# The branch for crowded experts goes into the loop of the experts, and the last expert's loads and down product are rearranged

## The chip, the cores and the metric

The kernel runs on one core of one Trainium2 chip. Its time is the device time of one execution, in microseconds (us). The time before is 2425.18 us, the median of 3 runs from 2423.32 to 2428.69. One further execution was recorded by the hardware profiler; it took 2428.05 us, and all durations below come from it.

The core has a matrix engine (PE, TensorE; its weight loads are PEld), VectorE (DVE), ScalarE (ACT), GpSimd (POOL) and SyncE (SP). SP computes nothing here: it issues nearly all DMA transfers, in the order of its program. A transfer that must wait (for a free buffer, say) holds back all that stand behind it on SP.

## The reference, cut to what matters

Two models of two layers run in one launch: a hybrid stack (recurrent and sparse attention, then multi-head latent attention, each with an mlp) on `x`, and two decoder layers on the second set of inputs (256 tokens, width 1024). What the change touches is the mixture of experts at the end of each decoder layer:

```python
def hier_moe(h, ...):          # 256 tokens, 32 experts in 4 groups, 2 experts per token
    ...                        # group by argmax, top 2 experts inside it, weights
    def expert_block(args):    # for the tokens of one expert e
        xb, e = args
        return (jax.nn.silu(xb @ w_exp_gate[e]) * (xb @ w_exp_up[e])) @ w_exp_down[e]
    ...
    return out                 # weighted sum over each token's two experts

x = x + gate2 * hier_moe(modulate(rms_norm(x), shift2, scale2))   # end of a layer
```

`w_exp_gate` and `w_exp_up` are 1024x512 per expert, `w_exp_down` 512x1024, all in float32: 2 MB each, 6 MB per expert, 192 MB per layer. The next layer begins with an rms norm of `x`, and after the second layer a final rms norm gives the output.

## The kernel before, in words

The experts are walked in order, 0 to 31. For each, up to 64 of its tokens are gathered beforehand (`xg`), and all 64 columns are computed whether they are filled or not. An expert that has more than 64 tokens is "crowded": a tensor `most` (the largest count) says whether there is one, and `crowded` (L1961) holds a loop over all experts for the tokens beyond the first 64, inside `tc.If(n > 64)` (L1967). Each engine loads the count into a register (L1966) and branches by itself. On the inputs timed here the body is not entered: the engines jump over it. Before the change this branch stands at the end of `moe`, behind everything else of the layer.

A weight matrix comes as two loads of 1 MB (128 partitions x 2048 numbers), issued by SP in `xload` (L1765, the DMA is at L1770). `xtile` deals out 17 buffers in turn: 7 called `xw`, 7 called `w`, 3 called `xw2`. So each load has to wait until PE has used the tile that was loaded 17 loads earlier, and for one of eight DMA semaphores (DMAHW0 to 7). The order of the loads is gate 0, up 0, and then for each expert e: gate e, down e-1, up e; at the end down 31. Counted from 0 in each layer, the loads of gate e, down e-1 and up e have the numbers 6e-2 to 6e+3.

PE's work per expert, in its program order: the gate product (`expert_in`, L1792, 32 passes for a matrix), the down product of the expert before (`expert_out`, L1816, 16 passes over 512 columns), the up product (L1792 again), `combine` (L1957, eight products that add the expert's output to four accumulators in PSUM), and two small transposes (`choice`, L1780; `expert_act`, L1804). Behind the down product ACT copies each half of the result out of PSUM (L1821) and DVE takes the rest of it to a second part (L1822); the two column halves c = 0 and 1 lie in one PSUM bank, in partitions 0 to 63 and 64 to 127.

At the end of a layer, in a block whose order is kept as written (`self.ordered()`), stand the last down product, its combine, the update of `x` (DVE, L1946), its squares (ACT, L1949), their sums (PE, L1950), and the scale of the next norm (`rstd_sums`, L461 to L471: a copy, a small product, a square root, a reciprocal). Then comes the branch, and then the next norm's first product (L478), which makes the scale available to all partitions.

Of the kernel before, what the change touches and what calls it, by code (L numbers as in the profile page):

```python
# [9 lines left out]
FT = mybir.dt.float32  # L10
FR = mybir.dt.float32r
# [3 lines left out]
AF = mybir.ActivationFunctionType  # L15
OP = mybir.AluOpType
# [4 lines left out]
T = 256  # L21
# [92 lines left out]
def layout(a):  # L114

    g = {}
# [5 lines left out]
    w = a["hy_w_in"][0]  # L122
    xr, yr, q, k, v, iq, ik, iw = np.split(w, np.cumsum([512, 512, 512, 64, 64, 256, 64])[:7], axis=1)
# [42 lines left out]
    for n, kc in (("w_exp_gate", 4), ("w_exp_up", 4), ("w_exp_down", 2)):  # L166
        g[n] = rowwise(a[n + "_2"], kc, 2048 // kc)[:, :, :, 0]
# [17 lines left out]
class Prog:  # L185
# [1579 lines left out]
    def xload(self, ap, kc, n):  # L1765

        half = []
        for h in range(2):
            t = self.xtile()
            self.nc.sync.dma_start(t, ap[h])  # L1770
            half.append(t.rearrange("p (c n) -> p c n", n=n))
        return lambda k: half[k // (kc // 2)][:, k % (kc // 2)]
# [36 lines left out]
    def expert_out(self, ht, wd):  # L1809

        nc = self.nc
        py = self.bank()
        for n in range(4):
            h, b = n // 2, n % 2
            for c in range(2):
                nc.tensor.matmul(py[64 * c:64 * c + 64], ht[:, b * 128 + h * 64:b * 128 + h * 64 + 64],  # L1816
                                 wd(2 * h + b)[:, c * 512:(c + 1) * 512], start=n == 0, stop=n == 3)
        y = self.t4("ey", FR)
        for c in range(2):
            p, n = py[64 * c:64 * c + 64], slice(c * 512, (c + 1) * 512)  # L1820
            nc.scalar.activation(y[:64, n], p, AF.Copy)  # L1821
            nc.vector.tensor_tensor(y[64:, n], p, y[:64, n].bitcast(FT), op=OP.subtract)  # L1822
        return y

    def moe(self, l):
# [88 lines left out]


        state = None
        for e in range(32):
            if e % G == 0:
                if e:
                    oh = onehot(e // G)  # L1920
                    xg = gather(oh, [[(k2, part)] for k2 in range(4) for part in range(2)])
                wohs = weighted(e // G, oh)
            xs = lambda k, xg=xg, a=e % G * 64: xg[k // 4][:, k % 4, a:a + 64]
            wg = self.xload(g["w_exp_gate"][l, e], 8, 512)
            ps = self.bank()
            self.expert_in(ps, 0, xs, wg)
            if state:
                wd = self.xload(g["w_exp_down"][l, e - 1], 4, 1024)
                y = self.expert_out(state[0], wd)
            wu = self.xload(g["w_exp_up"][l, e], 8, 512)  # L1930
            self.expert_in(ps, 256, xs, wu)
            if state:
                for j in range(8):
                    self.combine(acc, j, y, state[1], e == 1)
            ct, sw = self.choice(wohs[e % G])
            state = self.expert_act(ps, sw), ct
        gate = self.modc[:, l, 40:48]
        wd = self.xload(g["w_exp_down"][l, 31], 4, 1024)
        with self.ordered():
            self.table(AF.Sqrt, state[0][:, :1])  # L1940
            y = self.expert_out(state[0], wd)
            for j in range(8):
                self.combine(acc, j, y, state[1], False, True)
            sums = self.bank()
            for j in range(8):
                ve.scalar_tensor_tensor(self.x[j], acc[j // 2][:, (j % 2) * T:(j % 2 + 1) * T], gate[:, j:j + 1],  # L1946
                                        self.x[j], op0=OP.mult, op1=OP.add)
                sq = self.t1("rsq")
                sc.activation(sq, self.x[j], AF.Square)  # L1949
                te.matmul(sums[32 * (j % 4):32 * (j % 4) + 32, :T], self.ones[:, :32], sq, start=j < 4, stop=j >= 4)  # L1950
# [11 lines left out]
    def crowded(self, l, tok, posm, wt, most, gate, modulate):  # L1962
# [3 lines left out]
        n = nc.values_load(most[0:1, 0:1], min_val=0, max_val=T)  # L1966
        with tc.If(n > 64):  # L1967
            ev = self.sm.tile([128, 1], FT, name="ev", tag="ev", bufs=1)
            ve.memset(ev, 0.0)
            with tc.For_i(0, 32, 1) as e:  # L1970
                wts = []
                for n, kc, c in (("w_exp_gate", 4, 512), ("w_exp_up", 4, 512), ("w_exp_down", 2, 1024)):
                    half = []
                    for h in range(2):
                        w = self.ring.tile([128, 2048], FT, name="xw", tag="xw").rearrange("p (c n) -> p c n", c=kc)
                        rows = g[n][l, bass.ds(e, 1), h]
                        nc.sync.dma_start(w, rows.rearrange("e p (c n) -> p (e c) n", c=kc))
                        half.append(w)
                    wts.append(lambda k, half=half, kc=kc: half[k // kc][:, k % kc])
# [8 lines left out]
                for b in range(1, T // 64):  # L1988
# [20 lines left out]
                    for o in range(2):  # L2009
                        self.expert_in(ps, o * 256, lambda k: xg[:, k], wts[o])  # L2010
# [9 lines left out]
            self.rstd_tokens(self.squares(self.x), 8, 1e-6, out=self.r)  # L2020
# [129 lines left out]
```

## Time and profile before

| What | Before |
|---|---|
| Median of 3 runs | 2425.18 us (2423.32 to 2428.69) |
| Profiled execution | 2428.05 us, span 2426.2 us |
| PE busy | 2287.1 us (94%) |
| DVE, ACT, POOL busy | 1146.2 (47%), 868.7 (36%), 200.3 us (8%) |
| Moved by DMA | 658.71 MB, 272 GB/s over the span |
| Expert loop, layer 0 | about 1122 to 1566 us of the span |
| Expert loop, layer 1 | about 1958 to 2404 us of the span |

The shares are means over the whole program. The page also shows the span in 40 slices; in the slices of the two expert loops the DMA engines are busy 90% or more of the time at 420 GB/s, elsewhere mostly between 30 and 70%. So the two loops have to be read by themselves, and the rows further down do that. The time in the rows is that since the start of the span.

### The profile page before, as it was taken

Reading aid. Unit: us, or ns where it says so; the run is one execution under the profiler, and the core shown is the slowest. Engines: PE = TensorE matmul, PEld = TensorE weight load, DVE = VectorE, ACT = ScalarE, POOL = GpSimd, SP = SyncE. Lnnn points to the kernel's source line nnn. Section 1 sums busy time; section 2 is a strip of 40 time slices with the busy share of each in tenths; the row PEclk is TensorE's granted clock in tenths of the full one; section 3 lists DMA queues with packets and bytes.
Section 4 is the critical chain, followed back from the end, with each engine's and each line's share of the span. In section 5 each row is a group of like instructions: output and inputs, shape, how many; then the busy total and the mean of one; then the engine's idle time right before and its main releaser. Section 6 shows DMA issues by size and latency. Waiting matters only on the chain. (4 is left out here: it accounts for less than half of the span.)

```text
span 2426.2 us, 45869 instructions
## 1 busy us (share of the span) xinstructions
PE 2287.1 (94%) x19846; PEld 1816.3 (75%) x19846; DVE 1146.2 (47%) x1864; ACT 868.7 (36%) x1415; POOL 200.3 (8%) x171
## 2 busy tenths in 40 slices
PE   7899999999998999998889999889999988999996
PEld 7689997799997899986555565478989855565653
DVE  6775566665555756653222222258566432222222
ACT  4654445554445533442111221244335321121111
POOL 5110000010000101010000000010010100000000
PEclk9999999999999999999999999989999999999999
DMA  7745555555556534367999999955333679999996
GB/s 267 297 161 176 190 200 208 194 208 190 177 189 236 207 123 131 108 266 281 420 420 420 420 420 420 417 194 178 135 120 127 258 320 420 420 420 420 420 420 260
DMA packets 93315, 658.71 MB, mean 272 GB/s; under 512 B 10416, under 2 KB 11824, under 8 KB 14128
## 3 DMA queue, kind: packets, MB, share of 16 engines
q1 hardware_dynamic: 91376, 652.14, 69.3%
q10 hardware_dynamic: 1728, 3.54, 0.4%
q8 instruction: 159, 2.61, 0.4%
q14 instruction: 52, 0.43, 0.1%
HBM read 654.59 MB, written 1.05 MB: 270 GB/s over the span
## 5 line engine op out<-in xcount | busy, mean ns | idle before, releaser
L336 ACT ACTIVATE wh<-w 128x1024 fp32r<-128x1024 f32 x359 | 380.4, 1060 | 562.8 <-PE bank L353 494.3
L339 DVE TENSOR_TENSOR wl<-w,wh 128x1024 fp32r<-128x1024 f32 x330 | 420.1, 1274 | 334.3 <-ACT wh L336 333.4
L352 PE MATMUL bank<-hh,wh 128*128 128x256 f32 x1568 | 454.4, 290 | 0.0
L354 PE MATMUL bank<-hh,wl 128*128 128x256 f32 x1568 | 444.4, 283 | 3.5 <-DVE wl L339 3.5
L353 PE MATMUL bank<-hl,wh 128*128 128x256 f32 x1568 | 443.9, 283 | 0.0
L352 PEld LDWEIGHTS bank<-hh,wh 128*128 128x128 f32 x1568 | 300.7, 192 | 11.2 <-issue 7.9
L354 PEld LDWEIGHTS bank<-hh,wl 128*128 128x128 f32 x1568 | 301.0, 192 | 4.9 <-DVE wl L339 4.9
L353 PEld LDWEIGHTS bank<-hl,wh 128*128 128x128 f32 x1568 | 301.2, 192 | 1.1 <-issue 1.0
L1792 PE MATMUL bank<-xw,xg 128*64 128x256 f32 x2464 | 282.6, 381 | 2.3 <-SPq L1967 2.2
L1792 PEld LDWEIGHTS bank<-xw,xg 128*64 128x64 f32 x2464 | 173.3, 137 | 109.5 <-issue 22.9
L1822 DVE TENSOR_TENSOR ey<-bank,ey 64x512 fp32r<-64x512 f32 x128 | 88.2, 689 | 259.1 <-ACT ey L1821 259.1
L1792 PE MATMUL bank<-w,xg 128*64 128x256 f32 x1632 | 188.6, 381 | 5.4 <-DMA w<-in_w_exp_up_dram 5.4
L1792 PEld LDWEIGHTS bank<-w,xg 128*64 128x64 f32 x1632 | 114.2, 137 | 77.3 <-issue 13.8
L1821 ACT ACTIVATE ey<-bank 64x512 fp32r<-64x512 f32 x128 | 75.8, 592 | 264.1 <-PE bank L1816 216.4
L1785 DVE TENSOR_SCALAR ct<-cs 128x256 fp32r<-128x256 f32 x64 | 20.2, 316 | 304.2 <-ACT cs L1783 304.1
L1783 ACT ACTIVATE cs<-bank 128x256 f32<-128x256 f32 x64 | 24.5, 383 | 343.6 <-PE bank L1780 343.6
L1816 PE MATMUL bank<-xw,eh 128*64 128x512 f32 x608 | 143.2, 597 | 2.3 <-DVE eh L1806 1.0
L352 PE MATMUL bank<-rh,wh 128*128 128x256 f32 x512 | 144.9, 283 | 0.0
L353 PE MATMUL bank<-rl,wh 128*128 128x256 f32 x512 | 144.9, 283 | 0.0
L354 PE MATMUL bank<-rh,wl 128*128 128x256 f32 x512 | 144.9, 283 | 0.0
L1858 POOL TENSOR_TENSOR woh<-oh,wt 128x256 f32<-128x256 f32 x64 | 37.4, 615 | 750.0 <-PE bank L1792 526.1
L1816 PE MATMUL bank<-w,eh 128*64 128x512 f32 x416 | 97.9, 597 | 1.4 <-DMA w<-in_w_exp_down_dram 1.2
(526 smaller groups left out, 3885.5 us busy)
## 6 DMA issues: line engine op xcount, KB each, us to landing
xw<-in_w_exp_up_dram SPq DMA_DIRECT2D x78, 1024.0 KB, 17.3
xw<-in_w_exp_gate_dram SPq DMA_DIRECT2D x76, 1024.0 KB, 15.3
xw<-in_w_exp_down_dram SPq DMA_DIRECT2D x76, 1024.0 KB, 19.6
w<-in_mlp_w_dram SPq DMA_DIRECT2D x64, 1024.0 KB, 4.9
w<-in_w_exp_down_dram SPq DMA_DIRECT2D x52, 1024.0 KB, 17.1
w<-in_w_exp_gate_dram SPq DMA_DIRECT2D x52, 1024.0 KB, 15.9
w<-in_w_exp_up_dram SPq DMA_DIRECT2D x50, 1024.0 KB, 15.6
w<-in_w_ada_dram SPq DMA_DIRECT2D x48, 1024.0 KB, 4.9
```

The source lines that it names most:

```text
L336: nc.scalar.activation(hv, src, AF.Copy)
L339: (nc.gpsimd if fresh or pool else nc.vector).tensor_tensor(lv, src, hv.bitcast(FT), op=OP.subtract)
L352: te.matmul(out, a, xh[x0 + k], start=start and k == 0, stop=False, skip_group_check=True)
L353: te.matmul(out, a, xl[x0 + k], start=False, stop=False, skip_group_check=True)
L354: te.matmul(out, b, xh[x0 + k], start=False, stop=stop and k == kc - 1, skip_group_check=True)
L1783: nc.scalar.activation(s, pc[:, :T], AF.Copy, accum_out=w)
L1785: nc.vector.tensor_scalar(ct, s, 0.0, None, op0=OP.not_equal)
L1792: self.nc.tensor.matmul(ps[64 * h:64 * h + 64, o:o + 256], xk(k), w(k)[:, h * 256:(h + 1) * 256], start=k == 0 and o == 0, stop=k == 7, sk ...
L1816: nc.tensor.matmul(py[64 * c:64 * c + 64], ht[:, b * 128 + h * 64:b * 128 + h * 64 + 64], wd(2 * h + b)[:, c * 512:(c + 1) * 512], start=n ...
L1821: nc.scalar.activation(y[:64, n], p, AF.Copy)
L1822: nc.vector.tensor_tensor(y[64:, n], p, y[:64, n].bitcast(FT), op=OP.subtract)
L1858: nc.gpsimd.tensor_tensor(woh[:, i, :, c], oh[:, i].bitcast(FT), wt[:, i, es, None].to_broadcast([128, G, 64]), op=OP.mult)
```

## The change

The order of the loads is made by a list, and `weights()` takes the next pair of tiles from it. For expert 31 the order is gate, up, down 30, down 31 instead of gate, down 30, up, down 31.

After the combine of expert 9, SP first issues loads ahead until `turn` is a multiple of 17 (loads 58 to 67 of that layer), and then comes `crowded`, in the middle of the loop. Its buffers are taken out of the same pools ahead of the branch. It no longer computes the scale of the next norm itself.

The down matrices are stored so that one 1 MB tile holds 512 of the 1024 output columns for all of the inner dimension, where before it held half of the inner dimension for all columns. The down product is made of 32 passes over 256 columns instead of 16 over 512, one column half f after the other. For the last expert of a layer each half f is copied out, combined and added to `x` by itself. Both halves f lie in one PSUM bank.

```diff
-    def expert_out(self, ht, wd):
+    def expert_out(self, ht, wd, combine=None, add=None):
         py = self.bank()
-        for n in range(4):
-            h, b = n // 2, n % 2
+        pv = py.rearrange("p (f n) -> p f n", f=2)
+        y = self.t4("ey", FR)
+        yv = y.rearrange("p (f c n) -> p f c n", f=2, c=2)
+        def out(c, f):
+            p = pv[64 * c:64 * c + 64, f]
+            nc.scalar.activation(yv[:64, f, c], p, AF.Copy)
+            nc.vector.tensor_tensor(yv[64:, f, c], p, yv[:64, f, c].bitcast(FT), op=OP.subtract)
+        for f in range(2):
+            for n in range(4):
+                h, b = n // 2, n % 2
+                if combine and f and n == 2:
+                    combine(y, 0)
+                for c in range(2):
+                    nc.tensor.matmul(pv[64 * c:64 * c + 64, f], ht[:, b * 128 + h * 64:b * 128 + h * 64 + 64],
+                                     wd[f][:, 2 * h + b, c * 256:(c + 1) * 256], start=n == 0 and f == 0, stop=n == 3,
+                                     skip_group_check=True)
+            if combine:
+                if f:
+                    add(0)
+                for c in range(2):
+                    out(c, f)
+        if combine:
+            combine(y, 1)
+            add(1)
+        else:
             for c in range(2):
-                nc.tensor.matmul(py[64 * c:64 * c + 64], ht[:, b * 128 + h * 64:b * 128 + h * 64 + 64],
-                                 wd(2 * h + b)[:, c * 512:(c + 1) * 512], start=n == 0, stop=n == 3)
...
+                out(c, slice(0, 2))
         return y
...
+        for e in range(32):
+            down = [("down", e - 1)] if e else []
+            order += [("gate", e), *down, ("up", e)] if e < 31 else [("gate", e), ("up", e), *down]
+        order = iter(order + [("down", 31)])
...
+            if e == 9:
+                while self.turn % 17:
+                    load()
+                self.crowded(l, tok, posm, wt, most, gate, modulate)
             ct, sw = self.choice(wohs[e % G])
             state = self.expert_act(ps, sw), ct
...
-            y = self.expert_out(state[0], wd)
-            for j in range(8):
-                self.combine(acc, j, y, state[1], False, True)
-            sums = self.bank()
-            for j in range(8):
...
+            self.expert_out(state[0], wd, combine, add)
             self.r = self.rstd_sums(sums, 8, 1e-6)
         self.router_parts = None
-        self.crowded(l, tok, posm, wt, most, gate, modulate)
...
-            self.rstd_tokens(self.squares(self.x), 8, 1e-6, out=self.r)
```

The first place is SP in the first decoder layer, around loads 66 to 72. Before, they follow each other; `xw2_13237` is load 66, and each waits for its DMA semaphore and for PE's use of an earlier tile.

```order
L1770 DMA xw2_13237<-in_w_exp_down_dram 128x2048 [waits DMAHW6_49,PE_49]
L1770 DMA xw2_13239<-in_w_exp_down_dram 128x2048 [waits DMAHW7_49,PE_49]
L1770 DMA xw_13255<-in_w_exp_up_dram 128x2048 [waits DMAHW0_49,PE_49]
L1770 DMA xw_13257<-in_w_exp_up_dram 128x2048 [waits DMAHW1_49,PE_49]
L1770 DMA xw_13354<-in_w_exp_gate_dram 128x2048 [waits DMAHW2_49,PE_49]
L1770 DMA xw_13356<-in_w_exp_gate_dram 128x2048 [waits DMAHW3_49,PE_49]
L1770 DMA xw_13375<-in_w_exp_down_dram 128x2048 [waits DMAHW4_49,PE_49]
```

In the changed kernel the same loads 66 (`xw2_13203`) to 72 stand on both sides of the branch. The rows left out are the body, which reloads buffers of `xw` for the extra tokens.

```order
L1772 DMA xw2_13203<-in_w_exp_down_dram 128x2048 [waits DMAHW6_49,PE_49]
L1772 DMA xw2_13205<-in_w_exp_down_dram 128x2048 [waits DMAHW7_49,PE_49]
L2024 TENSOR_LOAD mosti_12199 [waits DVE_49]
L2032 COMPARE_AND_BRANCH
...
L2032 UNCONDITIONAL_BRANCH [waits DMAHW0_49,DMAHW1_49,DMAHW2_49,DMAHW3_49,DMAHW4_49,DMAHW5_49]
L2024 ISA x2
L1772 DMA xw_13776<-in_w_exp_up_dram 128x2048 [waits DMAHW0_49,PE_49]
L1772 DMA xw_13778<-in_w_exp_up_dram 128x2048 [waits DMAHW1_49,PE_49]
L1772 DMA xw_13876<-in_w_exp_gate_dram 128x2048 [waits DMAHW5_49,DMAHW2_49,PE_49]
L1772 DMA xw_13878<-in_w_exp_gate_dram 128x2048 [waits DMAHW4_49,DMAHW3_49]
L1772 DMA xw_13896<-in_w_exp_down_dram 128x2048
```

Load 68 (`xw_13776`) and those after it now stand behind the branch. The `PE_49` in their rows is a count of PE's instructions, and the counts have moved: load 68 waits for PE's use of tile 57 (before: of tile 51), and loads 69 and 70 wait for a count that PE reaches only when it has left the branch itself, since the buffers `xw` belong to the body too.

The second place is PE at the same point. In the changed kernel the combine of expert 8 (L2015) stands ahead of the branch, and the transposes of `choice` and the work of expert 10 (`w_13187` is load 58) behind it.

```order
L1799 MATMUL bank_13112<-xw_13161,xg_12970 64x256 x7
L2015 MATMUL bank_12201<-ct_13101,ey_13138 128x256 [waits DVE_49]
L2015 MATMUL bank_12201<-ct_13101,ey_13138 128x256
L2015 MATMUL bank_12202<-ct_13101,ey_13138 128x256 [waits DVE_49]
L2015 MATMUL bank_12202<-ct_13101,ey_13138 128x256
L2015 MATMUL bank_12203<-ct_13101,ey_13138 128x256 x2
L2015 MATMUL bank_12204<-ct_13101,ey_13138 128x256 x2
L2024 TENSOR_LOAD mosti_12199 [waits DVE_49]
L2032 COMPARE_AND_BRANCH
...
L2032 UNCONDITIONAL_BRANCH [waits PE_49]
L1787 MATMUL bank_13640<-con_161,woh_13015 128x128 [waits DVE_49,PE_49,Activation_49]
L1799 MATMUL bank_13657<-w_13187,xg_12969 64x256 [waits DMAHW6_49,PE_49]
```

So PE passes the branch between the last use of tile 57 (`xw_13161`) and the first use of tile 58, with the loads that SP has issued by then.

The third place is PE at the end of layer 0. Before, `xw_15250` and `xw_15252` are the two tiles of down 31, and the sums and the branch follow the combine.

```order
L1816 MATMUL bank_15258<-xw_15250,eh_15248 64x512 [waits DMAHW2_49,DVE_49]
L1816 MATMUL bank_15258<-xw_15250,eh_15248 64x512 x3
L1816 MATMUL bank_15258<-xw_15252,eh_15248 64x512 [waits DMAHW3_49]
L1816 MATMUL bank_15258<-xw_15252,eh_15248 64x512 x3
L1957 MATMUL bank_12201<-ct_15239,ey_15267 128x256 [waits DVE_49]
L1957 MATMUL bank_12201<-ct_15239,ey_15267 128x256
L1957 MATMUL bank_12202<-ct_15239,ey_15267 128x256 x2
L1957 MATMUL bank_12203<-ct_15239,ey_15267 128x256 [waits DVE_49]
L1957 MATMUL bank_12203<-ct_15239,ey_15267 128x256
L1957 MATMUL bank_12204<-ct_15239,ey_15267 128x256 x2
```

In the changed kernel `xw_15931` and `xw_15933` are these two tiles, `bank_15940` holds the result of both halves, `ey_15885` is the output of expert 30 and `ey_15941` that of expert 31.

```order
L1836 MATMUL bank_15940<-xw_15931,eh_15929 64x256 [waits DMAHW2_49,DVE_49]
L1836 MATMUL bank_15940<-xw_15931,eh_15929 64x256 x4
L2015 MATMUL bank_12202<-ct_15828,ey_15885 128x256 [waits DVE_49]
L2015 MATMUL bank_12202<-ct_15828,ey_15885 128x256
L2015 MATMUL bank_12203<-ct_15828,ey_15885 128x256 x2
L2015 MATMUL bank_12204<-ct_15828,ey_15885 128x256 x2
L1836 MATMUL bank_15940<-xw_15931,eh_15929 64x256 x3
L1836 MATMUL bank_15940<-xw_15933,eh_15929 64x256 [waits DMAHW3_49,DVE_49]
L1836 MATMUL bank_15940<-xw_15933,eh_15929 64x256 x3
L2015 MATMUL bank_12201<-ct_15920,ey_15941 128x256 [waits Activation_49]
L2015 MATMUL bank_12201<-ct_15920,ey_15941 128x256
L1836 MATMUL bank_15940<-xw_15933,eh_15929 64x256 x4
```

The first product of the second half now waits for DVE as well as for its load: DVE has to be through with the first half, which lies in the same bank. The combine of expert 30 has moved into the last down product.

## Rows read from the trace of the kernel before

**Rows 1.** Windows in both loops: engines' busy time, granted clock, DMA share, GB/s.

```profile
1150.00:1200.00 50.00, 45.25 (x346) 27.50 (x344) 12.22 (x23) 9.23 (x21) 2.37 (x4) 1.00 1.01 419
2300.00:2350.00 50.00, 48.34 (x360) 28.54 (x358) 10.85 (x22) 8.76 (x20) 2.33 (x4) 1.00 1.01 420
```

**Rows 2.** Timeline of PE near the end of layer 0's loop: start, duration, instruction, idle before.

```profile
1543.88 1.95 PE L1792 MATMUL bank<-w,xg 128*64 128x256 f32 x16 [0.55 <-DMA w<-in_w_exp_up_dram]
```

**Rows 3.** Timeline of PE around expert 9, layer 0: up product, combine.

```profile
1256.35 3.62 PE L1792 MATMUL bank<-xw,xg 128*64 128x256 f32 x32
1259.90 1.22 PE L1957 MATMUL bank<-ct,ey 128*128 128x256 f32 x8
```

**Rows 4.** Timeline of SP there: issues of loads 66 to 69.

```profile
1242.79 2.05 SPq L1770 DMA_DIRECT2D xw<-in_w_exp_down_dram  x2
1246.25 5.48 SPq L1770 DMA_DIRECT2D xw<-in_w_exp_up_dram  x2
```

**Rows 5.** DMA from 1244 to 1245 (load 67); last number: us from issue to landing.

```profile
xw<-in_w_exp_down_dram SPq DMA_DIRECT2D x1, 1024.0 KB, 10.3
```

**Rows 6.** DMA from 1251 to 1252 (load 69).

```profile
xw<-in_w_exp_up_dram SPq DMA_DIRECT2D x1, 1024.0 KB, 8.4
```

**Rows 7.** The page's DMA issues: 1 MB loads of the mlp, one at a time.

```profile
w<-in_mlp_w_dram SPq DMA_DIRECT2D x64, 1024.0 KB, 4.9
```

**Rows 8.** Line 1967, the branch: count, duration in ns (min/median/max), first and last start.

```profile
L1967 SPq COMPARE_BRANCH  x2: 50/50/50, 1556.7 to 2384.8; - x2
L1967 PEldq COMPARE_BRANCH  x2: 3899/5066/6234, 1577.2 to 2414.6; - x2
```

**Rows 9.** Line 1966, the load of the count on PE's sequencer.

```profile
L1966 PEldq TENSOR_LOAD <-mosti x2: 316/402/487, 1576.7 to 2414.2; - x2
```

**Rows 10.** Timeline of SP in layer 1: issues of loads 66 to 69.

```profile
2078.93 2.06 SPq L1770 DMA_DIRECT2D xw<-in_w_exp_down_dram  x2
2082.38 5.48 SPq L1770 DMA_DIRECT2D xw<-in_w_exp_up_dram  x2
```

**Rows 11.** DMA from 2080 to 2081 (layer 1, load 67).

```profile
xw<-in_w_exp_down_dram SPq DMA_DIRECT2D x1, 1024.0 KB, 11.4
```

**Rows 12.** DMA from 2087 to 2088 (layer 1, load 69).

```profile
xw<-in_w_exp_up_dram SPq DMA_DIRECT2D x1, 1024.0 KB, 9.5
```

**Rows 13.** Timeline of PE in layer 1: combine ahead of choice of expert 9.

```profile
2096.04 1.22 PE L1957 MATMUL bank<-ct,ey 128*128 128x256 f32 x8
```

**Rows 14.** DMA from 1546 to 1547: the last load of layer 0, issued at 1546.39.

```profile
xw<-in_w_exp_down_dram SPq DMA_DIRECT2D x1, 1024.0 KB, 19.9
```

**Rows 15.** Timeline of all engines at the end of layer 0.

```profile
1565.27 3.65 PE L1816 MATMUL bank<-xw,eh 128*64 128x512 f32 x16 [0.52 <-DVE eh L1806]
1569.03 0.59 ACT L1821 ACTIVATE ey<-bank 64x512 fp32r<-64x512 f32 x1 [3.49 <-PE bank L1816]
1569.65 0.68 DVE L1822 TENSOR_TENSOR ey<-bank,ey 64x512 fp32r<-64x512 f32 x1 [4.44 <-ACT ey L1821]
1570.37 0.59 ACT L1821 ACTIVATE ey<-bank 64x512 fp32r<-64x512 f32 x1 [0.75 <-DVE ey L1822]
1571.72 3.23 DVE L1946 SCALAR_TENSOR_TENSOR x<-bank,modc,x 128x256 f32<-128x256 f32 x8
1576.65 0.61 PE L468 MATMUL bank<-onesP,part 128*128 128x1 f32 x4 [0.52 <-DVE part L461]
1577.59 0.17 DVE L471 RECIPROCAL rstd<-rstd 128x2 f32<-128x2 f32 x1 [0.99 <-ACT rstd L470]
1583.79 0.66 PE L478 MATMUL bank<-con,rstd 128*128 128x128 f32 x2 [6.54 <-PEq L1967]
```

**Rows 16.** Timeline at the end of layer 1.

```profile
2415.11 0.17 DVE L471 RECIPROCAL rstd<-rstd 128x2 f32<-128x2 f32 x1 [0.99 <-ACT rstd L470]
2418.81 0.66 PE L478 MATMUL bank<-con,rstd 128*128 128x128 f32 x2 [4.04 <-PEq L1967]
```

**Rows 17.** Window behind layer 0: PE's busy time first, granted clock third from the end.

```profile
1580.00:1595.00 15.00, 7.52 (x39) 5.59 (x40) 10.16 (x14) 6.56 (x10) 5.65 (x2) 0.50 0.55 197
```

More of the change, by code (lines that the diff above doesn't have):

```diff
@@ L1 @@
+import itertools
 import math
@@ L1770, in xload, with rows @@
             self.nc.sync.dma_start(t, ap[h])
-            half.append(t.rearrange("p (c n) -> p c n", n=n))
-        return lambda k: half[k // (kc // 2)][:, k % (kc // 2)]
+            half.append(t.rearrange("p (c n) -> p c n", n=512))
+        return half
+    @staticmethod
+    def rows(half):
+        return lambda k: half[k // 4][:, k % 4]
     def choice(self, woh):
@@ L1913, in moe, with load, weights @@
         acc = [self.bank() for _ in range(4)]
+        gate = self.modc[:, l, 40:48]
+        order = []
+        for e in range(32):
+            down = [("down", e - 1)] if e else []
+            order += [("gate", e), *down, ("up", e)] if e < 31 else [("gate", e), ("up", e), *down]
+        order = iter(order + [("down", 31)])
+        ahead = []
+        def load():
+            n, e = next(order)
+            ahead.append(self.xload(g["w_exp_" + n][l, e]))
+        def weights():
+            if not ahead:
+                load()
+            return ahead.pop(0)
         state = None
@@ L1934, in moe, with combine, add @@
                     self.combine(acc, j, y, state[1], e == 1)
+            if e == 9:
+                while self.turn % 17:
+                    load()
+                self.crowded(l, tok, posm, wt, most, gate, modulate)
             ct, sw = self.choice(wohs[e % G])
             state = self.expert_act(ps, sw), ct
[L1937 to L1938 removed]
+        wd = weights()
         with self.ordered():
             self.table(AF.Sqrt, state[0][:, :1])
[L1941 to L1950 removed]
+            sums, sq = self.bank(), {}
+            def combine(y, f):
+                for j in range(4 * f, 4 * f + 4):
+                    self.combine(acc, j, y, state[1], False, True)
+            def add(f):
+                for j in range(4 * f, 4 * f + 4):
+                    ve.scalar_tensor_tensor(self.x[j], acc[j // 2][:, (j % 2) * T:(j % 2 + 1) * T], gate[:, j:j + 1],
+                                            self.x[j], op0=OP.mult, op1=OP.add)
+                    if j % 4 == 0:
+                        sq[f] = self.q4("rsq")
+                    sc.activation(sq[f][:, j % 4], self.x[j], AF.Square)
+                    if f:
+                        for k in (j - 4, j):
+                            te.matmul(sums[32 * (j % 4):32 * (j % 4) + 32, :T], self.ones[:, :32],
+                                      sq[k // 4][:, k % 4], start=k < 4, stop=k >= 4)
+            self.expert_out(state[0], wd, combine, add)
             self.r = self.rstd_sums(sums, 8, 1e-6)
         self.router_parts = None
[L1953 removed]
     def combine(self, acc, j, y, ct, start, stop=False):
@@ L1966, in crowded @@
         n = nc.values_load(most[0:1, 0:1], min_val=0, max_val=T)
+        bank, t1, t1r = (itertools.cycle(v) for v in (
+            [self.bank() for _ in range(3)], [self.t1("few") for _ in range(2)], [self.t1("few", FR) for _ in range(2)]))
+        t2, t4 = self.t2("xxg"), self.t4("xey", FR)
+        few = {"bank": lambda: next(bank), "t1": lambda name, dt=FT: next(t1 if dt == FT else t1r),
+               "t2": lambda name: t2, "t4": lambda name, dt: t4}
+        self.__dict__.update(few)
         with tc.If(n > 64):
```

35 lines of the change are left out of this document (17 added, 18 removed).

## The prediction

> **What bounds the kernel now.** I read first the table of windows in the two expert loops [rows 1]. The reader is to see that PE is busy 45 to 48 of 50 us at a full granted clock, and that the DMA engines are nevertheless the fuller resource: share 1.01, 419 to 420 GB/s, at the beginning of layer 0 as at the end of layer 1. A load of 1 MB (1,048,576 bytes) at 420 GB/s takes 2.50 us, so the six loads of an expert take 15.0 us. Second, PE's timeline near the end of a loop [rows 2]: it takes 1.95 us for a tile and has idled 0.55 us before it for the load of that very tile; 1.95 + 0.55 is the 2.50 us of a load. There PE eats tiles as they land, and the loop ends when its last load has landed.
>
> Around expert 9 it is otherwise. PE works on tiles 56 and 57 from 1256.35 to 1259.97 [rows 3]; load 69, the second of the pair whose issues end at 1246.25 + 5.48 [rows 4], so issued at 1251.40, lands 8.4 us later [rows 6], at 1259.8. So PE is 12 tiles, some 30 us of loading, behind the loads. It catches up in the experts that follow. A delay of PE there costs nothing as long as it is under 30 us; a pause of the loads cannot be made good, since nothing flows faster than 420 GB/s afterwards. So an interruption of the queue on SP in mid-loop is paid in full at the loop's end, twice.
>
> **The change part by part.** *The branch leaves the layer ends: -9.3 us.* In layer 0 the reciprocal ends at 1577.76 and PE's next product comes at 1583.79, put down to PE's sequencer at L1967 [rows 15]: 6.0 us, of which I leave 0.1 for the ordinary handover. In layer 1 it is 2418.81 - 2415.28 = 3.5, less 0.1 [rows 16]. 5.9 + 3.4 = 9.3. Both lie on the path: in layer 1 only the final norm follows. The branch instruction on PE took 3.9 and 6.2 us, on SP 50 ns [rows 8].
>
> *The branch arrives behind expert 8's combine: +21.1 us.* PE's own stall there (0.4 us for the count [rows 9] and 3.9 to 6.2 us [rows 8]) is far under 30 us and free. What is not free is what stands on SP. Loads 58 to 67 are issued ahead of the branch, at the times of before, since they wait for the same uses of tiles. Load 67, issued at 1242.79 + 2.05 less the 0.33 us of an issue, lands 10.3 us later [rows 4, 5], at 1254.8; then the queue is empty. Load 68, before issued at 1246.25 [rows 4], now waits until PE is through with tile 57, at 1259.97 [rows 3]. A 1 MB load into an idle queue takes 4.9 us [rows 7], so it lands at 1264.9. Load 69 waits for a count that PE reaches only when it has left the branch. The combine ends at 1261.1 [rows 3]. PE's sequencer runs a little ahead of its array: the count was loaded from 1576.7 [rows 9] while the last product ran until 1577.3 [rows 15], so I take 0.6 off, add 0.4 for the count and 5.1 for the branch (mean of the two), and get 1266.0. Load 69 then lands at 1270.9, where before it landed at 1259.8: 11.1 us. The loads behind it follow each 2.5 us, because their tiles are long used.
>
> In layer 1 load 67, issued at 2080.66, lands after 11.4 us [rows 10, 11]; load 69, issued at 2087.53, after 9.5 us, at 2097.0 [rows 10, 12]. PE's combine ends at 2097.26 [rows 13]; less 0.6, plus 0.4 and 5.1 it leaves the branch at 2102.2, and load 69 lands at 2107.1: 10.0 us (11.1 + 10.0 = 21.1 for both). Bounds: without any stall of PE, load 68 lands at 1264.9 and load 69 2.5 us behind, 7.6 us late; in layer 1 (tile 57 used just ahead of the combine's start, 2096.0) load 68 lands at 2101.0 and 69 at 2103.5, 6.5 us late; sum 14.1. With the long stall of 6.2 us in both layers 23.4; with the count and the branch each in their longest and another 2 us of refilling, 27. Nothing in the rows lets the gap vanish while the loads wait for the branch; that they may be hidden all the same is a rival below.
>
> The row on the branch shows 50 ns on SP and 3.9 to 6.2 us on PE for the same jump. The Trainium skill, "Runtime: NRT & Kernel Launch", section "Instruction fetch mechanics", says that a taken branch to a target outside the window of instructions already fetched waits for a fetch before execution goes on. The trace agrees so far as only PE, which has some 200 rows of body to jump, shows it. By that rule the stall comes along to the new place and the term is 21.1; if it belonged to the layer's end it would be 14.1.
>
> *The last expert's tail: +2.6 us.* The last load of layer 0, issued at 1546.39, lands 19.9 us later [rows 14], at 1566.3, and the reciprocal ends 11.5 us behind it [rows 15]. In that stretch stand a product of 3.65 us, begun before the landing, four evacuations in a chain (0.59, 0.68 and again, from 1569.03 to 1571.7), eight updates of x in 3.23 us and the rest of the norm. In the new order only the second half of the product (1.8 us) waits for the last load, and the updates of the first half can run beside it. Against that, the combine of expert 30 stands inside the first half's products; both halves share a bank, and the second half's first product waits for DVE's evacuation of the first. So PE, ACT and DVE take turns: my schedule by hand, with evacuations at 0.35 and 0.42 us (an estimate: half the width of those of 0.59 and 0.68, with their fixed part left), has the first half's evacuation end 2.9 us behind the landing, the second half's products with the combine between them 4.5, the second half's evacuation, which on ACT stands behind the four squares of the first, 7.5, the last four updates 9.2, and the reciprocal 12.3; in layer 0 ACT and DVE also have one piece of the next weights in between, and it is 13.3. So 1.8 and 0.8 us later, 2.6. From below, if the first half is wholly done when the last load lands: half of the updates (1.6) and 0.3 of the evacuations go, twice, -3.8. From above: each half evacuation at the price of a whole one, two more pairs of 1.3 us and a little, +3 per layer, +6.
>
> ACT's second copy waited 0.75 us for DVE [rows 15], although it reads other partitions of that bank. The Trainium skill, "PSUM — Partial Sum Buffer", section "PSUM bank collisions raise a hardware error", says that two engines must not be in one bank and quadrant of partitions at once. Both halves f use the same partitions of one bank, so by that rule the waiting is needed and the tail is the +2.6; in two banks it would be nearer to the lower bound. The trace agrees with the waiting.
>
> *The half clock behind layer 0: 0.* Behind the layer's end PE ran at a granted clock of 0.50, the lower level of 1.2 GHz, for 15 us with 7.52 us of work [rows 17], after thin work and the idle 6.5 us of the branch. If the clock stayed up without that idle time, half of that work, 3.8 us, would return. I take 0, because the sums of the norm, thin work too, stay.
>
> *The rest: 0.* The down product is 32 passes of half the width. The 32 passes over 256 columns of an up product take 3.62 us, the 16 over 512 take 3.65 [rows 3, 15]. Loads have the same size. The body of the branch is not entered. The load order of expert 31 is part of the tail.
>
> Sum: -9.3 + 21.1 + 2.6 = +14.4. The profiled execution took 2428.05, 2.9 over the median of 2425.2; on the median the sum gives 2439.6, and I say 2439.
>
> **The rivals.** First: PE's stall stays small at the new place, because it belonged to the layer's end. For it: SP's 50 ns. Against: both of PE's, in two layers, were long. The gap is then 14.1, the sum +7.4: 2432.6.
>
> Second, the other side: PE's lag absorbs the gap. PE has 12 tiles in hand at that place; if PE's work, and not the loads, set the end of the loop, a pause of 11 us in the loads would be eaten up unseen, and what remains is -9.3 + 2.6 = -6.7: 2418.5, faster. For it: PE is busy up to 48.3 of 50 us [rows 1]. Against: at the end it idles 0.55 us for each tile [rows 2], and 18 experts' idle time is what would be needed. It decides in its favour if a loop ends with PE still behind, by at least the gap.
>
> Third: the tail overlaps as meant and the clock comes back, with the full gap: -9.3 + 21.1 - 3.8 - 3.8 = +4.2, 2429.4.
>
> **How the numbers follow.** My forecast 62 in 100, the first rival 15, the third 9, the second 8; 6 for a larger gap or tail (the upper bounds together add 9.3, 2449). Within 0.2% of before, 4.9 us, is what a measurement can hardly tell from no change, 2420.3 to 2430.0. The second rival is faster; with a little from cases that mix, faster 0.08. The third falls inside, with some of the first's lower edge: same 0.11. Slower 0.81. The range goes from 2427, which takes in the third, to 2449, the upper bounds.
>
> **What would show it.** SP's timeline should have a pause between the issues of loads 67 and 68 of some 15 us, then another until PE leaves the branch; windows of 1250 to 1275 and 2088 to 2112 should show a DMA share well under 1, by 21 us of loads in all. PE should show a branch of 4 to 6 us there and none at the layer ends, with its next product some 0.2 us behind the reciprocal. PE should begin to wait for loads some experts earlier than before. If the DMA share stays at 1 through expert 9, or if the loop's last load lands as early as before, the forecast is wrong in its largest term; if the reciprocal comes less than 11 us after the last landing, the tail's sign is wrong.

## The result and the profile after

The changed kernel takes 2447.45 us (median of 5 runs, 2440.84 to 2448.83), beside 2425.18 for the one before (5 runs): a ratio of 1.0084, 95% interval 1.0073 to 1.0095, or 20 us more (18 to 23); the two medians alone are 22.3 apart. The forecast was 2439 in a range from 2427 to 2449, slower. The sign and the main mechanism were right; one term of the sum, the last expert's tail, had the right sign and a third of its size.

The table of windows of the changed kernel around expert 9 of layer 0, and below it two windows at the end of layer 1 (columns as in [rows 1]: the granted clock is third from the end, then DMA share and GB/s):

```profile
1240.00:1250.00 10.00, 8.54 (x76) 5.66 (x74) 2.51 (x5) 1.94 (x5) 0.00 (x0) 1.00 1.01 419
1250.00:1260.00 10.00, 10.00 (x94) 6.50 (x90) 1.45 (x3) 1.19 (x2) 0.00 (x0) 1.00 0.36 147
1260.00:1270.00 10.00, 4.75 (x26) 2.85 (x26) 2.72 (x7) 0.75 (x3) 0.00 (x0) 0.69 0.74 256
1270.00:1280.00 10.00, 10.00 (x90) 6.36 (x87) 1.38 (x2) 1.19 (x2) 0.00 (x0) 0.96 1.01 423
...
2425.00:2430.00 5.00, 3.50 (x20) 1.94 (x20) 2.50 (x6) 1.88 (x6) 0.00 (x0) 0.78 0.00 0
2430.00:2435.00 5.00, 3.99 (x21) 2.46 (x20) 2.58 (x6) 2.53 (x7) 0.00 (x0) 0.50 0.00 0
```

The loads stop while PE is fully busy (share 0.36 beside PE's 10.00 of 10): this is the pause, and it begins before PE reaches the branch. SP's timeline, which answers to [rows 4], shows why; its last two rows are the last loads of the two layers:

```profile
1242.93 2.05 SPq L1772 DMA_DIRECT2D xw<-in_w_exp_down_dram  x2
1260.16 5.10 SPq L1772 DMA_DIRECT2D xw<-in_w_exp_up_dram  x2
1265.37 1.61 SPq L1772 DMA_DIRECT2D xw<-in_w_exp_gate_dram  x2
...
1557.99 0.33 SPq L1772 DMA_DIRECT2D xw<-in_w_exp_down_dram  x1
...
2402.57 0.33 SPq L1772 DMA_DIRECT2D xw<-in_w_exp_down_dram  x1
```

Load 67 goes out at 1244.65, load 68 at 1260.16, load 69 at 1264.93. PE's timeline there, answering to [rows 3]:

```profile
1256.50 3.62 PE L1799 MATMUL bank<-xw,xg 128*64 128x256 f32 x32
1260.05 1.21 PE L2015 MATMUL bank<-ct,ey 128*128 128x256 f32 x8
1265.11 0.66 PE L1787 MATMUL bank<-con,woh 128*128 128x128 f32 x2 [3.85 <-PEq L2032]
```

Load 68 is issued as PE finishes tile 57 (1256.50 + 3.62 = 1260.12), and load 69 as PE comes out of the branch. The branch line of the changed kernel, in ns, beside [rows 8]:

```profile
L2032 SPq COMPARE_BRANCH  x2: 50/52/53, 1245.6 to 2070.1; - x2
L2032 PEldq COMPARE_BRANCH  x2: 3705/4234/4762, 1260.0 to 2105.7; - x2
```

The last loads took these times from issue to landing (layer 0, then layer 1; before: [rows 14]):

```profile
xw<-in_w_exp_down_dram SPq DMA_DIRECT2D x1, 1024.0 KB, 19.8
xw<-in_w_exp_down_dram SPq DMA_DIRECT2D x1, 1024.0 KB, 19.9
```

So layer 0's loads end at 1577.8, where they ended at 1566.3 before: 11.6 us later, from loops that began within 0.1 us of each other. In layer 1 the stretch from PE's first expert product to the last landing grew from 445.9 to 456.4 us, by 10.5.

The end of layer 0 in the changed kernel, all engines (before: [rows 15]):

```profile
1576.70 1.51 PE L1836 MATMUL bank<-xw,eh 128*64 128x256 f32 x10
1578.14 0.97 PE L2015 MATMUL bank<-ct,ey 128*128 128x256 f32 x6
1579.04 1.08 PE L1836 MATMUL bank<-xw,eh 128*64 128x256 f32 x6
...
1581.43 0.43 DVE L1828 TENSOR_TENSOR ey<-bank,ey 64x256 fp32r<-64x256 f32 x1 [0.45 <-ACT ey L1827]
1581.91 1.08 PE L1836 MATMUL bank<-xw,eh 128*64 128x256 f32 x8 [1.80 <-DVE ey L1828]
...
1583.60 1.08 PE L1836 MATMUL bank<-xw,eh 128*64 128x256 f32 x8
1585.76 0.38 ACT L1827 ACTIVATE ey<-bank 64x256 fp32r<-64x256 f32 x1
1587.49 1.66 DVE L1999 SCALAR_TENSOR_TENSOR x<-bank,modc,x 128x256 f32<-128x256 f32 x4
1592.76 0.16 DVE L473 RECIPROCAL rstd<-rstd 128x2 f32<-128x2 f32 x1
1592.98 0.43 PE L480 MATMUL bank<-con,rstd 128*128 128x128 f32 x2 [0.67 <-DVE rstd L473]
```

The last tile is there at 1577.8, and PE begins with it at 1581.91, after 1.80 us of waiting for DVE. PE's product on the scale follows the reciprocal at once (before: 6 us of branch in between). The same at the end of layer 1 (before: [rows 16]):

```profile
2428.43 1.98 PE L1836 MATMUL bank<-xw,eh 128*64 128x256 f32 x8
...
2437.81 0.17 DVE L473 RECIPROCAL rstd<-rstd 128x2 f32<-128x2 f32 x1 [1.40 <-ACT rstd L472]
2438.03 0.69 PE L480 MATMUL bank<-con,rstd 128*128 128x128 f32 x2 [0.55 <-DVE rstd L473]
```

Here the eight records that took 1.08 us in layer 0 take 1.98: the granted clock has fallen to 0.50 in the last window of the table, after PE's waits in the tail.

The two profiles add up: the loops are 22.1 us longer, the stretches from the last landing to the end of the reciprocal 7.6, the way from there to PE's next product is 9.5 shorter, and everything else 0.7 shorter. That is 19.5 us, the difference of the two spans (2445.7 and 2426.2).

### The profile page after: what moved, and what is told of

It reads as the page before. It is cut to its first block, busy times and chain, and to the rows that moved or that the text cites. A ratio compares the mean times of both kernels' runs of the same rounds, so it can differ in the third digit from the quotient of the medians.

```text
span 2445.7 us, 47906 instructions
## 1 busy us (share of the span) xinstructions
PE 2295.2 (94%) x20870; PEld 1896.6 (78%) x20870; DVE 1150.0 (47%) x1868; ACT 869.0 (36%) x1419; POOL 200.7 (8%) x171
## 5 line engine op out<-in xcount | busy, mean ns | idle before, releaser
L1828 DVE TENSOR_TENSOR ey<-bank,ey 64x512 fp32r<-64x512 f32 (+1 forms) x132 | 88.9, 673 | 298.2 <-ACT ey L1827 298.1
L1827 ACT ACTIVATE ey<-bank 64x512 fp32r<-64x512 f32 (+1 forms) x132 | 76.6, 580 | 310.5 <-PE bank L1836 241.0
L1836 PE MATMUL bank<-xw,eh 128*64 128x256 f32 x1216 | 146.2, 383 | 5.3 <-DVE ey L1828 3.6
L1836 PEld LDWEIGHTS bank<-xw,eh 128*64 128x64 f32 x1216 | 85.9, 137 | 51.3 <-issue 6.0
```

The lines of the kernel that those rows point to most:

```text
L1827: nc.scalar.activation(yv[:64, f, c], p, AF.Copy)
L1828: nc.vector.tensor_tensor(yv[64:, f, c], p, yv[:64, f, c].bitcast(FT), op=OP.subtract)
L1836: nc.tensor.matmul(pv[64 * c:64 * c + 64, f], ht[:, b * 128 + h * 64:b * 128 + h * 64 + 64], wd[f][:, 2 * h + b, c * 256:(c + 1) * 256], s ...
```

## The experiments

In us beside before, the ratio's interval times 2426. The changed kernel: +20.4 (17.7 to 23.0).

| Run | Branch | Tail | us against before |
|---|---|---|---|
| e1 | layer ends | changed | +8.7 (5.8 to 11.9) |
| e2 | expert 9 | of before | +7.5 (4.6 to 10.2) |
| e3 | none | changed | +0.7 (-1.5 to 2.9) |
| e4 | expert 26 | changed | +9.5 (6.1 to 12.6) |
| e5 | expert 17 | of before | +7.0 (4.6 to 9.2) |
| e6 | expert 17 | two banks | +4.4 (2.2 to 6.5) |
| e7 | expert 9, short body | changed | +12.9 (9.5 to 16.3) |
| e8 | none | of before | -9.0 (-12.4 to -5.6) |
| e9 | layer ends, rolled body | of before | -3.6 (-5.8 to -1.5) |
| e10 | layer ends, rolled body | two banks | -1.2 (-3.4 to 1.0) |
| e11 | none | two banks | -9.2 (-12.6 to -6.1) |
| e12 | layer ends, shorter body | of before | -2.9 (-5.1 to -0.7) |

**e1, the tail alone, and e2, the branch alone.** The changed kernel less one half of the change each.

```diff
 e1: -            if e == 9: ... self.crowded(...)
     +        self.crowded(...)                  # end of moe, as before
 e2: -        self.crowded(...)                  # in the kernel before
     +            if e == 9: ... self.crowded(...)
```

> The branch stands at the layer ends as before; load order, column halves and the split tail are those of the changed kernel. Theory (the gap in the loop costs 22 us, the branch's going gives back 9.5, the split tail costs 7.6, by the profiles of the two kernels): 2425.2 + 7.6 = 2432.8 us. Rival (the split tail costs 2.6 us as forecast, and the other 5 us are an effect of the branch in the loop): 2427.8 us. If the halves overlapped as written: 2421.4 us.

> Only the branch moves behind the combine in the pass of expert 9, with the loads issued ahead; load order, down product and tail are those of before. Theory: 2425.2 - 9.5 + 22 = 2437.7 us, DMA idle about 11 us in each loop. Rival (split tail costs 2.6, branch the rest): 2442 to 2443 us. If PE's lag of 30 us covered the gap: 2415.7 us.

e1 came out as the theory said: the tail costs more than the forecast, without any branch in the loop. It is not quite the tail alone: in its profile the two tails are 6.6 us longer than before and the loops 2.7, while PE's branch in layer 0 is 2.5 shorter. e2 is under both numbers that had a gap in them. Its profile shows the parts of the theory, loops 20.4 us longer and 9.3 given back at the layer ends; what is missing lies mostly ahead of the first expert product (1118.6 us, before 1121.7), which the edit does not touch. Both halves of the change lose by themselves.

**e3 and e8, no branch at all,** with the changed tail and with that of before.

```diff
 e3: -            if e == 9: ... self.crowded(...)
 e8: -        self.crowded(...)                  # in the kernel before
```

> The changed kernel without the branch and its body: the tokens of crowded experts beyond 64 are left out. Theory: no gap, so 2425.2 - 9.5 + 7.6 = 2423.3 us. Rival (split tail costs 2.6): 2418.3 us. The difference from the changed kernel is what the branch in the loop costs: 24 us by the medians if the gap is all of it.

> Before without the branch and its body (tokens of crowded experts beyond 64 are left out). Theory: the two idle stretches at the layer ends are all that the branch cost before, 6.5 and 3.4 us: 9.9 us under before, some 2416 us. If ACT and DVE have the next weights ready only later, so that part of it was hidden: 3 to 6 us under before.

e8 is what the branch costs where it stood before: 9.0 us, the two idle stretches of [rows 15, 16]. e3 is 2.6 us over its theory's number, just outside its interval. e3 less e8 is the tail by itself, 9.7 us (e1 says 8.7), with some 4 us of uncertainty either way. For the branch in the loop by itself there are two numbers: e2 less e8, 16.5 us, and the changed kernel less e3, 19.7. The profiles show what spreads them, and why e3 missed: without any pause, the two loops took 447.6 and 447.0 us in e8 and 447.1 and 447.4 in e3, where before they took 444.5 and 445.9. So these differences can't be read more finely than a few us.

**e4 and e5, the branch at other experts.**

```diff
-            if e == 9:
+            if e == 26:     # e4
+            if e == 17:     # e5, with the tail of before, and ahead of the loop:
+        self.turn = 3       # e5: so that the seven xw buffers are free there
```

> The changed kernel with the branch in the pass of expert 26 instead of 9. There PE is only about 1 us behind the loads, 8 to 9 loads are issued and not landed, and loads 160 to 169 are ahead of the branch. Theory (what costs is that the queue runs dry while SP waits for PE): 20 us of queued loads cover the 5 us of PE's branch, PE catches up 2.4 us per expert in the last five; 2423 to 2427 us, no window with a DMA share under 0.9. Rival (the branch costs its stall wherever it stands in the loop, all the more where PE has no lag): 2423.3 + 2 x 5 = 2433 us or more.

> Load order, down product and tail of before; the branch behind the combine in the pass of expert 17, the rotation of the buffers begun at 3 so that the seven xw buffers are free there. PE is some 17 us behind the loads at that place (28 at expert 9, 1 at 26). Theory (the loads pause where PE's lag is longer than the ten loads issued ahead, and PE's own stall is free where 1.8 us of catching up per expert are left for it): a gap of 1 to 3 us per layer and PE just in time at the end; 9.9 less, 2 to 6 more, so 4 to 8 us under before, some 2420 us. Rival (a branch in the loop costs about 9 us per layer wherever it stands, as at 9 and at 26): 8 to 10 us over before, some 2435 us.

Half of the theory held: with the queue full or PE less far behind, the loads do not pause. In e4 the DMA share (next to last number) stays at 1.01 through the branch of layer 0, and the last load of that layer lands at 1568.2; in e5 at 1567.6:

```profile
1490.00:1500.00 10.00, 3.31 (x17) 1.66 (x17) 1.20 (x3) 0.75 (x3) 0.00 (x0) 0.62 1.01 415
```

But e4 is as slow as its rival said, and e5 nearly so (7.0 us, where 8 to 10 stood), for a reason that neither theory had: now PE is late. PE's timeline of e4 at the branch:

```profile
1489.04 1.22 PE L2015 MATMUL bank<-ct,ey 128*128 128x256 f32 x8
1495.54 0.66 PE L1787 MATMUL bank<-con,woh 128*128 128x128 f32 x2 [5.28 <-PEq L2032]
...
1579.66 1.08 PE L1836 MATMUL bank<-xw,eh 128*64 128x256 f32 x8 [1.81 <-DVE ey L1828]
```

PE begins with the last tile of layer 0 11.4 us after its landing; in the changed kernel it is 4.1. At expert 26 there is too little left in which to catch up. In e5 there should have been enough. PE's timeline there at the branch and four experts later:

```profile
1375.72 0.66 PE L1781 MATMUL bank<-con,woh 128*128 128x128 f32 x2 [5.12 <-PEq L1990]
...
1439.89 0.44 PE L1805 MATMUL bank<-con,em 128*128 128x128 f32 x2 [1.47 <-DVE em L1802]
```

In before, from expert 10 on, the scheduler has put `choice` between the two tiles of the down product, and its way over ACT and DVE is covered. Behind the branch it starts afresh, and `choice` stands behind the combine again for six or seven experts in layer 0: PE idles 1.4 to 1.8 us for DVE in each. PE used the last tile 10.5 us after its landing. So a branch in the loop has a second price, paid in the order of what follows; at expert 9 PE has time for it.

Layer 1 is the control. There PE idles so only once behind the branch, and in e5 the scale's reciprocal ends 12.4 us behind the last landing (before: 11.5), in layer 0 21.3; in e4 17.7 and 24.1. So in layer 1 of e5 the theory came true, and its loss sits in layer 0.

**e7, a short body.** PE jumps over 18 products instead of some 200 rows.

```diff
-                sel = ...                        # gather, choice, all products, updates of x
+                for o in range(2):
+                    for k in range(8): te.matmul(ps[:64, ...], xg[:, k], wts[o]...)
+                for w in wts[2]: te.matmul(ps[64:, :256], xg[:, 0], w[:, 0, :256], ...)
+                ve.tensor_tensor(self.x[0], self.x[0], ps[:, :T], op=OP.add)
```

> The changed kernel with a short body under the branch (the six loads of an expert, 18 products and one addition; what it would compute for crowded experts is left out). PE jumps over some 20 rows instead of 200. Theory (PE's stall is the fetch of a far target): PE's branch takes under 1 us, the pause of the loads shrinks from 9.3 and 8.6 us of lost loading to 6 to 7, and the kernel is 4 to 7 us faster than the changed one. Rival (a branch costs PE 4 us whatever it jumps over): no difference from the changed kernel, 2447 us.

The branch line of e7 (ns):

```profile
L2032 PEldq COMPARE_BRANCH  x2: 228/300/371, 1260.3 to 2099.7; - x2
```

As the theory said: with a jump this short PE's stall is gone, and the kernel is 7.5 us faster than the changed one, some 4 us either way. Not all of that is the pause. Counted from load 57's to load 69's landing, as it is below, it shrank from 10.2 to 9.2 us in layer 0 and from 8.7 to 6.4 in layer 1, where the theory had 6 to 7; at the last landings e7's loops are 0.5 and 5.0 us shorter than the changed kernel's. The first rival's world, a small stall at the new place, is thus 12.9 us slower than before, since the wait for tile 57 and the refilling of the queue remain.

**e6, e10 and e11, two banks.** The last expert's column halves each in their own bank, both multiplied ahead of any combine, all evacuations ahead of the updates of x.

```diff
-            for f in range(2): products f, with combine(y, 0) inside f = 1; add(0); evacuate f
+            for f in range(2): self.half(py[f][:, :256], state[0], wd[f], True)
+            for f in range(2): evacuate f; combine(f)
+            for f in range(2): add(f)
```

> The branch as in the run before (expert 17), the load order and column halves of the changed kernel, but in the last expert each column half has a PSUM bank of its own, both halves are multiplied before anything is combined, and all evacuations come before the updates of x. Theory (the split tail loses because the halves take turns in one bank and behind the updates on ACT): the tail is 1 to 1.5 us shorter per layer than that of before, so 2 to 3 us under the run before. Rival (any split of the last product costs, by its added evacuations and combines): 3 to 7 us over the run before.

> The two-bank tail without any branch (tokens of crowded experts beyond 64 are left out), to be held against the run with the old tail and no branch (9 us under before) and that with the changed tail and no branch (1 us over before). Theory (one bank, and evacuations queued behind the squares, are what the changed tail loses): 2 to 3 us under the old tail's, so 11 to 12 under before, some 2414 us; the reciprocal 10 to 10.5 us behind the last landing in both layers. Rival (the added evacuations and combines cost by themselves): 3 to 7 us over the old tail's, 2419 to 2424 us.

> The run before with the load order, column halves and two-bank tail of the run e6: the branch at the layer ends with the shorter body. Theory (two banks shorten the tail by 1 to 1.5 us per layer): 2 to 3 us under the run before. Rival (a split tail costs): 3 to 7 us over it.

The reciprocals of e11:

```profile
1578.94 0.17 DVE L473 RECIPROCAL rstd<-rstd 128x2 f32<-128x2 f32 x1 [0.99 <-ACT rstd L472]
...
2413.03 0.17 DVE L473 RECIPROCAL rstd<-rstd 128x2 f32<-128x2 f32 x1 [0.99 <-ACT rstd L472]
```

Both start 10.2 us behind the last landing (1568.7 and 2402.8), as expected; in before, and in e8, it is 11.4, in e1 and e3 14.5 to 14.7. So the split tail of the change loses by its arrangement and not by being split. The bank and the order were changed together, so the share of each is open. The 2.4 us that the profile gives do not show in the times: e11 and e8 are level, e6 is under e5 by 2.6 with overlapping intervals, and e10 is not under e9 (its PE branch in layer 1 took 3.4 us, e9's 0.4). In the profiles e11's loop in layer 1 took 2.2 us more than e8's, and PE is late in layer 0 of e6 as in e5.

**e9 and e12, a shorter body at the old place.** Before, with the loop over a crowded expert's further blocks made a loop of the machine (e9), and with seven products fewer in the body (e12).

```diff
-                for b in range(1, T // 64):
+                with tc.For_i(1, T // 64, 1):              # e9, e12
...
-            self.rstd_tokens(self.squares(self.x), 8, 1e-6, out=self.r)
+            ...                                            # e12: add the squares on DVE,
+            s, m = self.partial([sq[0]], 1)                # then one product for their sum
```

> Before, the branch left at the layer ends; only the loop over a crowded expert's further blocks of 64 tokens, written out three times under the branch, becomes a loop of the machine, so that PE's jump spans some 95 rows instead of 200. Theory (PE's stall is the fetch of a far target, and grows with or sets in at the length of the jump): if 95 rows are near enough, PE's branch falls from 3.9 and 6.2 us to under 1 and the kernel is 7 to 9 us faster than before, 2417 to 2419 us; if the stall is proportional to the rows, 4 to 5 us faster. Rival (only a body as short as the 20 rows of the run with a short body is near enough): no difference.

> The run with the rolled body (3 us under before, PE's branch 6.1 us in layer 0 and 0.4 us in layer 1), with seven products fewer under the branch: the squares are added up by VectorE first. Theory (what a jump costs PE is decided by whether its target lies in a block of instructions that has been fetched already; layer 0's jump went just past the end of the next block, and 14 instructions fewer bring it inside): PE's branch under 1 us in both layers, 8 to 9 us under before, some 2418 us. Rival (it is a matter of the length of the jump alone, or of chance): a stall of 3 to 6 us stays in layer 0, 3 to 5 us under before.

The branch lines of e9 and of e12 (layer 1's is the short one in both):

```profile
L1967 PEldq COMPARE_BRANCH  x2: 363/3255/6147, 1577.1 to 2411.1; - x2
```

```profile
L1967 PEldq COMPARE_BRANCH  x2: 363/3298/6234, 1576.5 to 2413.3; - x2
```

e9 beats both kernels, 3.6 us under before, and leaves none of the work out: layer 1's stall is gone, layer 0's is not. That is between e9's theory (7 to 9) and its rival (no difference). The idea behind e12, that 14 instructions decide, fell: the stall in layer 0 stayed, as its rival said.

## Why the prediction was right, and where it was not

*What bounds the kernel.* Right: the loads set the end of the loops, and a pause in them in mid-loop was paid at the end, 11.6 us in layer 0. The second rival (PE's lag absorbs the gap) is out. e4 and e5 show where it would have turned: later in the loop the lag is short, and the price moves to PE. One of the prediction's signs did not come: PE was to begin waiting for loads some experts earlier. Before, it waited from 1499 us on in layer 0; in the changed kernel it waits once, at 1570.5. The order behind the branch used up its time, so that it was nearly the limit itself. Its waits from 1400 to 1580:

```profile
PE bank L1836 <- DMA xw<-in_w_exp_down_dram: 0.6, 1, 0.6
```

The prediction's "0.55 us for each tile" was not a reading of all tiles: around [rows 2] PE idles for some of an expert's six, and the 18 experts can't be worked out from the rows named.

*The branch leaves the layer ends, -9.3.* Right: 9.0 by e8, and in the changed kernel's profile PE follows the reciprocal within 0.1 us.

*The branch in the loop, +21.1.* Right in its mechanism: the issue of load 68 at tile 57's last use (forecast 1259.97 plus nothing, measured 1260.16), of load 69 as PE leaves the branch. Into the idle queue load 68 took longer than the 4.9 us of [rows 7], 6.6 us in layer 0 and 5.4 in layer 1, but load 69 set the gap. Load 69 landed at 1270.1 (forecast 1270.9), 10.3 us late; in layer 1 the stretch from load 57's to load 69's landing grew from 29.9 to 38.6 us, 8.7 where 10.0 stood. The difference is mostly PE's branch: 4.8 and 3.7 us, not the mean of 5.1. The mean was the wrong row: the pause has emptied the load queue when PE branches, as it was empty in layer 1 of before (3.9); the last section shows what this does. At the last landings the term is 11.6 + 10.5 = 22.1 us, by the times 16.5 (e2 less e8) or 19.7 (the changed kernel less e3). The fetch rule of the Trainium skill, "Runtime: NRT & Kernel Launch", section "Instruction fetch mechanics", was the one to follow: the stall came along with the jump, and in e7 it went with the jump's length.

*The tail, +2.6.* This step failed in its size. The reciprocal ends 15.1 us (layer 0) and 15.5 us (layer 1) behind the last landing, where 13.3 and 12.3 stood and 11.5 was before: 7.6 us, above even the upper bound of 6; 8.7 by e1, 9.7 by e3 less e8, and 6.6 and 6.3 in the tails of their profiles. The term that was mis-sized is "the second half's products with the combine between them 4.5": from 2.9 that leaves 1.6 us for them, while the rows I had gave half of a product of 3.65 and half of a combine of 1.22 [rows 3, 15], 2.4 together. Measured, they run from 1581.91 to 1584.68, 2.8 us. The first half was late too: its products with the combine of expert 30 take from 1576.70 to 1580.12, and its evacuation ends 4.0 us behind the landing, not 2.9. These two, 1.2 and 1.1 us, are more than the 1.8 by which layer 0 missed; the steps behind them were a little shorter than forecast. In layer 1 the half clock adds its part (1.98 us for 1.08), which I had priced only for the stretch behind layer 0. The prediction's other half, that two banks would bring the tail near the lower bound of -3.8, fits e11: 1.1 us less than before in each layer, -2.3, though the order was changed with the banks. The 0.75 us of [rows 15] were a wait between different partitions of a bank; the wait that the two halves brought is the 1.80 us above.

*The half clock.* Taken at 0, and near it. Behind layer 0 the granted clock was 0.89 from 1580 to 1595, where it was 0.50 before [rows 17], but then 0.66 to 1610; the stretch from PE's product on the scale to layer 1's first expert product became 1.0 us shorter, not 3.8. What the prediction had no term for are two other places. In layer 1's tail the clock fell some 5 us behind the last landing, before only behind the reciprocal; e1 and e3, with the same tail, kept it longer, so the tail alone does not explain it. And behind the branch at expert 9 the first 32 passes took 5.1 us, not 3.6; there PE's lag hides it.

The sum of +14.4 was low by 6 us, 5 of them the tail and 1 the loops (22.1 for 21.1).

## What to carry to other kernels

A branch belongs where the engine that issues the loads does not have to wait for the slowest engine to leave it: what costs in a loop bound by loads is not the branch's microseconds but the dry queue behind it, and its body's buffers decide which loads wait. Before moving a branch, make its body shorter (roll its loops): over 18 products PE did not stall, over some 95 rows only sometimes. And take the price of a stall from a row where the same things run beside it: PE's cost about 4 us beside a dry load queue and 6 beside a full one. When a last product is split to overlap its tail, give the halves different banks and write the order out with the durations of the rows, engine by engine, before believing in the overlap.

## What the runs showed of the hardware

PE's jump over some 200 rows took 5.9 to 6.2 us where the loads were running as it began (both layers of e4, e5 and e6, layer 0 of before: DMA share 0.8 or more in its first two microseconds), and 3.4 to 4.8 us where the queue was dry or running dry (the changed kernel, e1, e2, layer 1 of before: at most 0.5 in the first). The body of about 95 rows cost 6.0 to 6.2 us in layer 0, with the loads running, and in layer 1, with none, 0.4 (e9, e12) or 3.4 (e10). Over 18 products it took 0.2 to 0.4 us.

The traces show a fetch of instructions behind this. In every stall of 3.4 us or more, one packet of 16 KB moves on a DMA queue for instructions that the profile calls q8. In the short stalls it starts 0.9 to 1.3 us after the jump, in the long ones 3.4 to 3.7, and PE goes on 1.4 to 1.6 us after the packet's end. In the jumps of 0.2 to 0.4 us there is none. The queue's rows (packets, MB, share of the window), first the changed kernel in layer 0, in the first 2 us of its 4.8:

```profile
q8 instruction: 1, 0.02, 7.1%
```

Then e4 in layer 0, where the first 3 us of its 6.2 have no packet on q8 and the other 3.2 have it:

```profile
q1 hardware_dynamic: 171, 1.25, 100.3%
q14 instruction: 1, 0.01, 0.6%
...
q1 hardware_dynamic: 176, 1.29, 98.7%
q8 instruction: 1, 0.02, 2.3%
```

And e9 in layer 1, its whole 0.4 us:

```profile
DMA packets 0, 0.00 MB, mean 0 GB/s; under 512 B 0, under 2 KB 0, under 8 KB 0
```

So the state of the load queue goes with how long the stall is. Why the same shorter body needs a packet in layer 0 and, in e9 and e12, none in layer 1 stays open: the place of the target in the program and the running loads were not varied apart.

The loops without a pause lose up to 1.6 us of loading now and then. In e1, where loads 68, 115 and 163 landed 3.6 to 3.7 us after the one before instead of 2.5, this came every 118 to 121 us; what causes it is open. Whole loops without a pause differ by 3 to 4 us between kernels with the same loads (444.5 to 447.6 us in layer 0, 445.3 to 449.2 in layer 1).
